# Softmax weights normalised ahead of their transposes, in a two-layer hybrid attention trunk on one core

## The chip, the core and the metric

The kernel is one program on one core of a Trainium2 chip. The metric is the device time of the program in microseconds (us); before the change its median over three runs is 1350.64 us (1348.82 to 1351.12). All times are in us unless marked ns. Engines: PE (TensorE, matrix products and transposes, with PEld its weight loads), DVE (VectorE), ACT (ScalarE), POOL (GpSimd), SP (SyncE, which issues the DMAs).

## What is computed

Two layers over 512 tokens of width 1024. Each layer normalises x, projects it once into the heads of five attention branches (four heads of 64 each), and merges the five results by sigmoid gates. Four branches take a softmax, whose weights are divided by their row sum:

```
e = jnp.where(mask, jnp.exp(l - m), 0.0)
return e / jnp.maximum(jnp.sum(e, axis=-1, keepdims=True), 1e-30)
...
y = (softmax weights) @ v, times the SiLU gate z of the branch
```

A attends to the keys that a top-k leaves, B to all earlier keys with a forget bias, E to 256 memory tokens. D runs three softmaxes (compressed keys, selected blocks, window) and adds their results, each times a sigmoid gate per token and head: `g0*o_cmp + g1*o_slc + g2*o_win`. C is a stick-breaking branch without a softmax; the change doesn't touch it.

## The kernel before

**Stages.** Every layer runs the branches as Python generators that `weave` interleaves with projections and merges, so that PE always has large products beside the attention. In the stretch that matters here the order is: E (`mem_attn`) with the merge of C, the projections of D and the first half of the top-k; D (`nsa_attn`) with the merge of E, the projections of A and the rest of the top-k; A (`dsa_attn`) with the merge of D and B's projections; B (`fox_attn`) with the merge of A; the merge of B alone. The projections and merges write the tile `pj`; their weights come in by DMA (`wraw`), are split by ACT into `whi` (L269) and by DVE into `wlo` (L270), and multiply in three products of 128 by 512 each.

**Order.** A scheduler lays the instructions of each engine out once, when the program is built; on the chip each engine takes its own list strictly in order and waits on semaphores where an operand is not there. A late operand therefore holds everything behind it on that engine.

**A head in a causal branch (A, B, D).** `causal` (L575 on) goes over four blocks of 128 queries and four heads. PE writes the scores into a bank S (two banks). `softmax_p` (L541) then lets DVE add the mask and find the maximum (L546, with its accumulator read), and ACT take the exponential and the row sum (L547, with its accumulator read). Two heads later (`lag` is 2) `finish` transposes the weights P on PE (`pt`, L556), ACT or DVE copy them to SBUF (L537, L539), and after the fourth head `pv_pair` multiplies them with V into a bank Y, which holds features on partitions and tokens on columns.

**Division.** Y is not yet divided. `inv_sums` (L605) takes the reciprocal of the four sums on DVE. They lie one per token on partitions, while Y has tokens on columns, so `head_rows` (L611) spreads them to 256 columns (ACT for A, B and E at L616; DVE for D at L618, times the gate) and transposes them on PE, two transposes into a bank `hr` (L621). `gated_y` (L637) multiplies `hr` by the SiLU gate Z (L640) and Y by that (L642). In D each of two parts (selected, window) has its own Y, `hr`, copy (L1183) and product (L1185); the compressed part comes from two products into a bank `oc`, and three passes of DVE add and gate (L1193 to L1196). Banks Y, `pt`, `hr` and `oc` share three banks (tag T).

**E.** `mem_attn` works on pairs of heads: scores, maximum (L1273), exponential (L1274), transposes and products with V follow at once for each pair.

Of the kernel before, what the change touches and what calls it, by code (L numbers as in the profile page):

```python
# [21 lines left out]
T = 512  # L22
# [164 lines left out]
def trunk(ctx: ExitStack, tc: tile.TileContext, xt, memt, pos, wall, small, vec, ca, cb, out):  # L187
# [373 lines left out]

    def pv_pair(Y, pr, V, PTs, nblk, last):

        after_qk = recent[-1] if last is None else None
        for j in range(nblk):
            for e in (1, 0):
                m = mm(Y[64 * e:64 * e + 64, pr], V(e, j), PTs[e][:, 128 * j:128 * j + 128], j == 0, j == nblk - 1)
                after(m, last, after_qk)
                last, after_qk = m, None
        return last  # L570

    def causal(blocks, lag):

        pend = []
        for i, scores, sums, mask, V, done in blocks:  # L575
            n = 128 * (i + 1)
            st_ = {"P": [], "PT": []}

            share = (4, 2, 1, 1)[i]
            for h in range(4):  # L580
                S = bank("S", "S")
                scores(h, S[:, :max(n, 256)], slice(128 * i, 128 * i + 128), slice(0, max(n, 256)))
                P = softmax_p(S[:, :n], n, mask, sums[:, h:h + 1])

                def finish(i=i, h=h, n=n, P=P, V=V, done=done, st_=st_, share=share):
                    st_["P"].append(P)
                    if len(st_["P"]) == share:
                        PT = transposed(st_["P"], share * (i + 1))
                        st_["PT"] += [PT[:, n * k:n * k + n] for k in range(share)]
                        st_["P"] = []  # L590
                    if h == 3:
                        Y = bank("Y", "T", (128, 2, 128))
                        last = None
                        for pr in (1, 0):
                            last = pv_pair(Y, pr, lambda e, j: V(2 * pr + e, j), st_["PT"][2 * pr:], i + 1, last)
                        done(Y)

                pend.append(finish)
                if len(pend) > lag:
                    pend.pop(0)()  # L600
                yield
        for f in pend:
# [7 lines left out]

    def head_rows(r, gate=None):  # L611

        rb_ = sm.tile([128, 4, 64], F32, name="rb_", bufs=1)
        rr = r[:, :, None].to_broadcast([128, 4, 64])
        if gate is None:
            nc.scalar.activation(rb_, rr, AF.Copy)  # L616
        else:
            nc.vector.tensor_mul(rb_, rr, gate[:, :, None].to_broadcast([128, 4, 64]))  # L618
        p = bank("hr", "T", (128, 2, 128))
# [65 lines left out]
    def layer(l, xs, begin):  # L685
# [122 lines left out]
        def small_proj():  # L808
# [35 lines left out]
            for h in range(4):  # L844
# [5 lines left out]
                for i in range(1, NB):  # L850
# [5 lines left out]
                    else:  # L856
                        R = wk.tile([128, T], F32, name="R", tag="P", bufs=3)[:, :n]
# [72 lines left out]
        def sb_attn(pr):  # L930
# [12 lines left out]
            def begin(e, j):  # L943
# [10 lines left out]
                t = wk.tile([128, T], F32, name="sp_t", tag="P", bufs=3)[:, :w]  # L954
# [90 lines left out]
        def plain_attn(scores, mask, V, Z, Yhl):  # L1045
            def blocks():
                for i in range(NB):
                    sums = sm.tile([128, 4], F32, name="sums", bufs=4)
# [384 lines left out]
```

## Time and profile before

| | |
|---|---|
| median of three runs | 1350.64 us |
| the profiled execution | 1351.01 us |
| its span, first to last instruction | 1349.2 us |
| PE busy | 1310.1 us (97%), 7240 matmul instructions |
| DVE busy | 892.8 us (66%), 1847 |
| ACT busy | 689.0 us (51%), 1300 |
| POOL busy | 11.4 us (1%), 28 |
| granted TensorE clock | 0.997 of full speed, so the 2.4 GHz level |

How to read it: matmuls are pipelined, so the busy time of one overlaps that of the next; what one costs PE is the distance between two starts in the order of time. A wait is the idle time in front of an instruction, put down to what ended it. The chain of work that ended last is followed back from the last instruction.

### The profile page before, as it was taken

What the parts mean: (1) busy time and instruction counts of PE and PEld (TensorE: products, weight loads), DVE (VectorE), ACT (ScalarE), POOL (GpSimd) and SP (SyncE); (2) the same over time, 40 slices, a digit from 0 to 9 for tenths busy, and PEclk for the clock granted to TensorE, in tenths of its full rate; (3) what the DMA queues carried; (4) which work ended last, traced back from release to release, by engine and by line L of the source; (5) the groups of instructions that cost most, each with busy time, mean ns of one, the idle gap of its engine ahead of it and who ended that gap; (6) DMA issues with size and microseconds to landing.
All of it is one profiled execution on the core that took longest, in us unless ns stands there. A gap on an engine that the chain in (4) does not pass through costs nothing.

```text
span 1349.2 us, 18962 instructions
## 1 busy us (share of the span) xinstructions
PE 1310.1 (97%) x7240; PEld 1068.4 (79%) x7240; DVE 892.8 (66%) x1847; ACT 689.0 (51%) x1300; POOL 11.4 (1%) x28
## 2 busy tenths in 40 slices
PE   7999999999999999999999999999999999999997
PEld 6777777878888788878887777777788778887896
DVE  6887999767655444545567799995676463454554
ACT  6887834357545434434447795534574452343340
POOL 0000000000000000000000000000000000000000
PEclk9999999999999999999999999999999999999998
DMA  6442321321123132224524313222122222323231
GB/s 215 139 127 77 110 78 63 94 78 59 63 79 102 55 94 78 71 84 130 183 81 126 109 63 110 85 68 84 57 69 63 86 86 66 100 77 103 94 111 63
DMA packets 40235, 124.11 MB, mean 92 GB/s; under 512 B 4432, under 2 KB 6480, under 8 KB 40144
## 3 DMA queue, kind: packets, MB, share of 16 engines
q1 hardware_dynamic: 40144, 122.89, 28.5%
q8 instruction: 57, 0.93, 0.3%
q14 instruction: 34, 0.28, 0.1%
HBM read 118.16 MB, written 4.72 MB: 91 GB/s over the span
## 4 chain that ended last, share of the span: by engine, by line
PE 70%; ACT 6%; DVE 5%; issue 2%; DVEq 0%; ACTq 0%
PE pj L259 58%; PE Y L259 3%; PE S L259 3%; PE pt L556 3%; ACT whi L269 2%; DVE wlo L270 1%; PE hr L621 1%; ACT sw L430 1%; ACT sw L431 1%; PE sbz L259 1%; DVE P L546 0%; ACT P L547 0%; DVE score L902 0%; DVE m L901 0%; ACT Qi L848 0%
## 5 line engine op out<-in xcount | busy, mean ns | idle before, releaser
L259 PE MATMUL pj<-h_hi,whi 128*128 128x512 f32 x1088 | 429.5, 396 | 0.7 <-DVE rt L433 0.7
L259 PE MATMUL pj<-h_hi,wlo 128*128 128x512 f32 x1088 | 429.0, 394 | 0.0
L259 PE MATMUL pj<-h_lo,whi 128*128 128x512 f32 x1088 | 429.0, 394 | 0.0
L270 DVE TENSOR_TENSOR wlo<-wraw,whi 128x1024 fp32r<-128x1024 f32 x183 | 223.7, 1223 | 228.1 <-ACT whi L269 217.0
L269 ACT ACTIVATE whi<-wraw 128x1024 fp32r<-128x1024 f32 x183 | 193.4, 1058 | 319.9 <-PE pj L259 213.9
L259 PEld LDWEIGHTS pj<-h_hi,wlo 128*128 128x128 f32 x1088 | 204.5, 188 | 42.8 <-DVE wlo L270 2.3
L259 PEld LDWEIGHTS pj<-h_hi,whi 128*128 128x128 f32 x1088 | 204.6, 188 | 40.5 <-issue 1.7
L259 PEld LDWEIGHTS pj<-h_lo,whi 128*128 128x128 f32 x1088 | 204.6, 188 | 40.4 <-issue 1.8
L547 ACT ACTIVATE P<-P,nm 128x128 f32<-128x128 f32 (+3 forms) x128 | 71.6, 559 | 67.7 <-DVE nm L546 64.2
L259 PE MATMUL pj<-yhi,whi 128*128 128x512 f32 (+1 forms) x192 | 71.9, 374 | 2.9 <-ACT yhi L269 2.9
L259 PE MATMUL pj<-yhi,wlo 128*128 128x512 f32 (+1 forms) x192 | 71.6, 373 | 0.0
L259 PE MATMUL pj<-ylo,whi 128*128 128x512 f32 (+1 forms) x192 | 71.5, 372 | 0.0
L556 PE MATMUL pt<-CA,P 128*128 128x128 f32 x384 | 62.7, 277 | 2.6 <-ACT P L1274 1.3
L546 DVE CUSTOM_DVE_ANT_0 P<-S,CA 128x128 f32<-128x128 f32 (+3 forms) x104 | 47.6, 468 | 18.1 <-PE S L259 18.0
L556 PEld LDWEIGHTS pt<-CA,P 128*128 128x128 f32 x384 | 44.9, 141 | 18.2 <-ACT P L1274 6.0
L259 PE MATMUL S<-Ks,Qs 128*128 128x256 f32 (+2 forms) x160 | 51.0, 358 | 6.6 <-DVE nm L546 6.5
L394 ACT ACTIVATE G<-pj 128x512 f32<-128x512 f32 x92 | 53.6, 582 | 0.3
L902 DVE MATCH_REPLACE8 score<-m,score 128x256 f32<-128x256 f32 (+2 forms) x96 | 51.7, 541 | 0.0
L901 DVE MAX8 m<-score 128x8 f32<-128x256 f32 (+2 forms) x96 | 49.7, 546 | 0.0
L799 DVE SCALAR_TENSOR_TENSOR G<-G,pj 128x512 f32<-128x512 f32 x64 | 43.6, 681 | 3.6 <-PE pj L259 3.3
L800 DVE TENSOR_TENSOR acc<-acc,G 128x512 f32<-128x512 f32 x64 | 44.0, 688 | 0.9
L259 PEld LDWEIGHTS pj<-yhi,whi 128*128 128x128 f32 x192 | 36.2, 188 | 10.4 <-ACT yhi L269 4.0
(478 smaller groups left out, 2006.1 us busy)
## 6 DMA issues: line engine op xcount, KB each, us to landing
wraw<-in_wall_dram SPq DMA_DIRECT2D x192, 512.0 KB, 3.7
wc<-in_wall_dram SPq DMA_DIRECT2D x16, 256.0 KB, 6.1
x<-in_xt_dram SPq DMA_DIRECT2D x8, 256.0 KB, 7.0
mraw<-in_memt_dram SPq DMA_DIRECT2D x4, 512.0 KB, 4.7
xo<-in_xt_dram SPq DMA_DIRECT2D x8, 256.0 KB, 4.3
xspill<-xn SPq DMA_DIRECT2D x8, 256.0 KB, 2.2
xo<-xspill SPq DMA_DIRECT2D x8, 256.0 KB, 4.0
out_dram<-o SPq DMA_DIRECT2D x8, 256.0 KB, 2.2
```

The costliest lines, as they stand in the source:

```text
L259: return nc.tensor.matmul(out_, lhsT, rhs, start=start, stop=stop, **kw)
L269: nc.scalar.activation(hi, raw, AF.Copy)
L270: nc.vector.tensor_sub(lo, raw, hi.bitcast(F32))
L394: i = nc.scalar.activation(*a, **k)
L430: nc.scalar.activation(sw[a], p[b], AF.Copy)
L546: nc.vector.tensor_tensor_reduce(P, S, mask, -1.0, 3e38, OP.add, OP.min, nm)
L547: nc.scalar.activation(P, P, AF.Exp, bias=nm, scale=-1.0, accum_out=sums)
L556: nc.tensor.transpose(pt[:, 128 * j:128 * j + 128], x[:, c:c + 128], ident)
L799: nc.vector.scalar_tensor_tensor(G, G, gc, p, op0=gop, op1=OP.mult)
L800: nc.vector.tensor_add(acc, acc, G)
L901: nc.vector.max(m8, lv.work[i])
L902: nc.vector.match_replace(lv.work[i], m8, lv.work[i], REPL)
```

## The change

The division moves from Y to P. In A, B and D each head's weights are multiplied on DVE by the reciprocal of their sum (in D also by the gate of their part), in `normalise` (L594, L595), whose call stands behind the next head's `softmax_p`. `head_rows` goes, with its transposes and the passes that used them. Y is multiplied by Z alone (L648). D's two parts and the compressed part add up in one bank Y, which is taken at the first part and read after the last. In E the weights are multiplied on POOL (L1270), the sums are inverted for two heads at a time, and transposes and products come a pair of heads later. P has four buffers where it had three.

```diff
     def softmax_p(S, n, mask, sums):
-        P = wk.tile([128, T], F32, name="P", tag="P", bufs=3)[:, :n]
+        P = wk.tile([128, T], F32, name="P", tag="P", bufs=4)[:, :n]
...
     def causal(blocks, lag):
-        for i, scores, sums, mask, V, done in blocks:
+        pend, norm_ = [], []
+        for i, parts, rest, done in blocks:
...
+            for b, (scores, mask, V, gate) in enumerate(parts):
+                sums = sm.tile([128, 4], F32, name="sums", bufs=4)
+                for h in range(4):
...
+                    Ps.append(softmax_p(S[:, :n], n, mask, sums[:, h:h + 1]))
+                    if norm_:
+                        norm_.pop()()
+                    def normalise(x=Ps[h], s=sums[:, h:h + 1], g=None if gate is None else gate[:, h:h + 1]):
+                        nc.vector.reciprocal(s, s)
+                        nc.vector.tensor_scalar(x, x, s, g, op0=OP.mult, **({} if g is None else dict(op1=OP.mult)))
+                    norm_.append(normalise)
...
+                            if not more:
+                                if rest is not None:
+                                    rest(st_["Y"], last)
+                                done(st_["Y"])
...
-    def head_rows(r, gate=None):
-        rb_ = sm.tile([128, 4, 64], F32, name="rb_", bufs=1)
...
-        for pr in range(2):
-            nc.tensor.transpose(p[:, pr], rb_[:, 2 * pr:2 * pr + 2].rearrange("p h d -> p (h d)"), ident)
-        return p
...
-    def gated_y(i, Y, r, Z, Yhl):
-        rows = head_rows(r)
-        g = yt("g")
-        nc.vector.tensor_mul(g, rows, Z[:, :, 128 * i:128 * i + 128])
+    def gated_y(i, Y, Z, Yhl):
         y = yt("y")
-        nc.vector.tensor_mul(y, Y, g)
+        nc.vector.tensor_mul(y, Y, Z[:, :, 128 * i:128 * i + 128])
...
         def nsa_attn():
+                    def rest(Y, last, i=i):
+                        for pr in range(2):
+                            m = mm(Y[:, pr], lv.vcb[:, 128 * pr:128 * pr + 128], lv.PC[:, 128 * i:128 * i + 128], False, pr == 1,
+                                   skip_group_check=True)
...
         def mem_attn():
+                    r = inv_sums(sums, 2)
+                    for e in range(2):
+                        x = P[:, NM * e:NM * e + NM]
+                        nc.gpsimd.tensor_scalar(x, x, r[:, e:e + 1], None, op0=OP.mult)
+                    def finish(i=i, pr=pr, P=P, st_=st_):
+                        PT = transposed(P, 4)
...
+                    pend.append(finish)
+                    if len(pend) > 1:
+                        pend.pop(0)()
```

How the instructions move, at three places. First PE in E, first layer, second pair of heads of the second block (S are scores of one head, `pt` takes the transposes of P, `pj` projections). Before, the scores of the pair and what follows:

```order
L259 MATMUL pj_1908<-yhi_1088,wlo_1628 128x512
L259 MATMUL S_1925<-KE_945,Qs_1174 128x256
L259 MATMUL S_1925<-KlE_946,Qs_1174 128x256
L259 MATMUL S_1931<-KE_945,Qs_1177 128x256
L259 MATMUL S_1931<-KlE_946,Qs_1177 128x256
L259 MATMUL pj_1968<-h_hi_384,whi_1964 128x512
L259 MATMUL pj_1968<-h_lo_385,whi_1964 128x512
```

Now, at the same place:

```order
L259 MATMUL pj_1902<-yhi_1088,wlo_1621 128x512
L259 MATMUL S_1920<-KE_945,Qs_1174 128x256
L259 MATMUL S_1920<-KlE_946,Qs_1174 128x256
L259 MATMUL S_1926<-KE_945,Qs_1177 128x256
L259 MATMUL S_1926<-KlE_946,Qs_1177 128x256
L556 MATMUL pt_1937<-CA_95,P_1836 128x128 x4
L259 MATMUL pj_1955<-h_hi_384,whi_1951 128x512
L259 MATMUL pj_1955<-h_lo_385,whi_1951 128x512
```

Before, the transposes of this pair's P_1924 came eleven and twelve projections behind its scores. Now those of the pair before (P_1836) stand there, and those of this pair come 78 projections later.

Second PE in D, first layer, end of a block of two (Y takes the products with V, PC and vcb are the compressed part). Before:

```order
L259 MATMUL S<-Ks,Qs 128x384
L259 MATMUL Y<-PT,VSW 64x128 x8
L621 MATMUL hr<-CA,rb__3318 128x128 x2
L259 MATMUL oc<-PC,vcb 128x128 x2
L259 MATMUL S<-Kl,Qs 128x384
L259 MATMUL S<-Ks,Qs 128x384
L556 MATMUL pt<-CA,P 128x128 x3
L259 MATMUL S<-Kl,Qs 128x384
L556 MATMUL pt<-CA,P 128x128 x3
L259 MATMUL S<-Ks,Qs 128x384
L259 MATMUL S<-Kl,Qs 128x384
```

Now:

```order
L259 MATMUL S<-Ks,Qs 128x384
L259 MATMUL Y<-PT,VSW 64x128 x8
L259 MATMUL Y<-PC,vcb 128x128 x2
L259 MATMUL S<-Kl,Qs 128x384
L556 MATMUL pt<-CA,P 128x128 x3
L259 MATMUL S<-Ks,Qs 128x384
L259 MATMUL S<-Kl,Qs 128x384
L556 MATMUL pt<-CA,P 128x128 x3
```

The two transposes `hr` are gone, and the products that went to `oc` go to Y, right behind its own; the scores and transposes of the next heads follow in nearly the same order.

Third DVE in B, second layer, last block (P<-S is mask and maximum; `wlo`, G and acc belong to weights and merge). Before:

```order
L800 TENSOR_TENSOR acc<-acc,G 128x512
L539 COPY PT<-pt 128x384
L546 ISA P,nm<-S,CA 128x512
L546 ISA nm 128x1
L640 TENSOR_TENSOR g<-hr,Z 128x256
L642 TENSOR_TENSOR y<-Y,g 128x256
L270 TENSOR_TENSOR ylo<-y,yhi 128x2x128
L270 TENSOR_TENSOR wlo<-wraw,whi 128x1024
L799 SCALAR_TENSOR_TENSOR G<-G,pj 128x512
```

Now:

```order
L546 ISA P,nm<-S,CA 128x512
L546 ISA nm 128x1
L806 TENSOR_TENSOR acc<-acc,G 128x512
L539 COPY PT<-pt 128x384
L546 ISA P,nm<-S,CA 128x512
L546 ISA nm 128x1
L594 RECIPROCAL sums<-sums 128x1
L595 TENSOR_SCALAR P<-P,sums 128x512
L594 RECIPROCAL sums<-sums 128x1
L648 TENSOR_TENSOR y<-Y,Z 128x256
L595 TENSOR_SCALAR P<-P,sums 128x512
L270 TENSOR_TENSOR ylo<-y,yhi 128x2x128
```

The product with `hr` is gone; two reciprocals and two scalings stand behind the second head's maximum, ahead of the copies and splits of the merge.

## Rows read from the trace of the kernel before

**Rows 1.** The page, busy time of each engine (share of the span, instructions).

```profile
PE 1310.1 (97%) x7240; PEld 1068.4 (79%) x7240; DVE 892.8 (66%) x1847; ACT 689.0 (51%) x1300; POOL 11.4 (1%) x28
```

**Rows 2.** The page, the chain that ended last, by line.

```profile
PE pj L259 58%; PE Y L259 3%; PE S L259 3%; PE pt L556 3%; ACT whi L269 2%; DVE wlo L270 1%; PE hr L621 1%; ACT sw L430 1%; ACT sw L431 1%; PE sbz L259 1%; DVE P L546 0%; ACT P L547 0%; DVE score L902 0%; DVE m L901 0%; ACT Qi L848 0%
```

**Rows 3.** Waits of PE: us in total, times, longest us.

```profile
PE S L259 <- DVE nm L546: 6.5, 11, 0.9
...
PE pt L556 <- ACT P L1274: 1.3, 2, 0.6
```

**Rows 4.** PE in order of time, behind Y: start us, us, instruction.

```profile
189.58 0.44 PE L621 MATMUL hr<-CA,rb__1951 128*128 128x128 f32 x2
189.77 0.47 PE L259 MATMUL pj<-h_lo,whi 128*128 128x512 f32 x1
```

**Rows 5.** PE in order of time, between projections.

```profile
228.30 0.39 PE L259 MATMUL pj<-h_lo,whi 128*128 128x512 f32 x1
...
228.75 0.39 PE L259 MATMUL pj<-h_hi,whi 128*128 128x512 f32 x1
228.99 0.38 PE L621 MATMUL hr<-CA,rb__2263 128*128 128x128 f32 x2
...
229.44 0.40 PE L259 MATMUL pj<-h_hi,wlo 128*128 128x512 f32 x1
```

**Rows 6.** PE in order of time, ahead of transposes of P.

```profile
317.20 0.44 PE L621 MATMUL hr<-CA,rb__3162 128*128 128x128 f32 x2
317.48 0.38 PE L556 MATMUL pt<-CA,P 128*128 128x128 f32 x2
```

**Rows 7.** Chain in order of time, twelve transposes: start us, us.

```profile
498.17 1.31 PE pt L556 x12
```

**Rows 8.** Groups by line, PE's weight loads: busy us, mean ns | idle before.

```profile
L556 PEld LDWEIGHTS pt<-CA,P 128*128 128x128 f32 x384 | 44.9, 141 | 18.2 <-ACT P L1274 6.0
```

**Rows 9.** Groups by line and form, DVE: busy us, mean ns | idle before.

```profile
L608 DVE RECIPROCAL rsum<-rsum 128x4 f32<-128x4 f32 x40 | 6.9, 171 | 0.8
...
L640 DVE TENSOR_TENSOR g<-hr,Z 128x256 f32<-128x256 f32 x24 | 10.1, 422 | 24.8 <-PE hr L621 24.7
...
L546 DVE CUSTOM_DVE_ANT_0 P<-S,CA 128x512 f32<-128x512 f32 x24 | 16.3, 682 | 7.7 <-PE S L259 7.7
...
L905 DVE TENSOR_SCALAR score<-score 128x512 f32<-128x512 f32 x2 | 0.8, 418 | 0.0
...
L905 DVE TENSOR_SCALAR score<-score 128x256 f32<-128x256 f32 x2 | 0.5, 274 | 0.0
...
L871 DVE TENSOR_SCALAR fu<-v,VEC 32x512 f32<-32x512 f32 x2 | 1.0, 486 | 0.1
```

**Rows 10.** Groups by line and form, ACT.

```profile
L547 ACT ACTIVATE P<-P,nm 128x512 f32<-128x512 f32 x32 | 23.0, 720 | 21.6 <-DVE nm L546 20.7 <-DVE rsum L607 1.0
...
L547 ACT ACTIVATION_READ_ACCUMULATOR P<-P,nm 128x1 f32 x128 | 24.0, 187 | 0.0
...
L1274 ACT ACTIVATE P<-S,nm 128x256 f32<-128x256 f32 x32 | 15.0, 471 | 21.7 <-DVE nm L1273 21.3
```

**Rows 11.** Busy time by stretch: length, PE, PEld, DVE, ACT, POOL, clock, DMA.

```profile
150.00:200.00 50.00, 49.60 (x312) 37.63 (x311) 48.82 (x119) 24.46 (x48) 0.00 (x0) 1.00 0.32 105
...
450.00:500.00 50.00, 49.71 (x288) 42.38 (x288) 18.77 (x31) 17.73 (x30) 0.00 (x0) 1.00 0.21 64
```

**Rows 12.** Groups by line, DVE, 150 to 250 us alone.

```profile
L902 DVE MATCH_REPLACE8 score<-m,score 128x512 f32<-128x512 f32 (+2 forms) x45 | 24.2, 542 | 0.0
...
L270 DVE TENSOR_TENSOR wlo<-wraw,whi 128x1024 fp32r<-128x1024 f32 x13 | 15.8, 1218 | 0.4
L1273 DVE TENSOR_REDUCE nm<-S 128x1 f32<-128x256 f32 x14 | 5.6, 414 | 0.6 <-PE S L259 0.5
```

**Rows 13.** Groups by line, POOL.

```profile
L476 POOL MEMSET Ks<- 64x512 f32 x16 | 8.7, 545 | 932.5 <-PE S L259 389.8 <-DVE sq L683 386.7 <-issue 61.1
L476 POOL MEMSET KlE<- 64x256 f32 x8 | 2.4, 306 | 15.2 <-ACT sq L336 8.4 <-DVE h_lo L270 6.5
```

More of the change, by code (lines that the diff above doesn't have):

```diff
@@ L560, in transposed, with pv_pair @@
         return o
-    def pv_pair(Y, pr, V, PTs, nblk, last):
-        after_qk = recent[-1] if last is None else None
+    def pv_pair(Y, pr, V, PTs, nblk, last, hold, first, end):
         for j in range(nblk):
             for e in (1, 0):
-                m = mm(Y[64 * e:64 * e + 64, pr], V(e, j), PTs[e][:, 128 * j:128 * j + 128], j == 0, j == nblk - 1)
-                after(m, last, after_qk)
-                last, after_qk = m, None
+                m = mm(Y[64 * e:64 * e + 64, pr], V(e, j), PTs[e][:, 128 * j:128 * j + 128], first and j == 0, end and j == nblk - 1,
+                       skip_group_check=True)
+                after(m, last, hold)
+                last, hold = m, None
@@ L570, in pv_pair @@
         return last
     def causal(blocks, lag):
-        pend = []
-        for i, scores, sums, mask, V, done in blocks:
+        pend, norm_ = [], []
+        for i, parts, rest, done in blocks:
             n = 128 * (i + 1)
-            st_ = {"P": [], "PT": []}
+            st_ = {"Y": None}
             share = (4, 2, 1, 1)[i]
[L580 to L601, printed above, removed]
@@ L602, in causal, with finish @@
-        for f in pend:
+            for b, (scores, mask, V, gate) in enumerate(parts):
+                sums = sm.tile([128, 4], F32, name="sums", bufs=4)
+                Ps = []
+                pt_ = {"P": [], "PT": []}
+                for h in range(4):
+                    S = bank("S", "S")
+                    scores(h, S[:, :max(n, 256)], slice(128 * i, 128 * i + 128), slice(0, max(n, 256)))
+                    Ps.append(softmax_p(S[:, :n], n, mask, sums[:, h:h + 1]))
[5 more added lines that the diff above has]
+                    norm_.append(normalise)
+                    def finish(i=i, h=h, b=b, n=n, Ps=Ps, V=V, rest=rest, done=done, st_=st_, pt_=pt_, share=share, more=b + 1 < len(parts)):
+                        pt_["P"].append(Ps[h])
+                        if len(pt_["P"]) == share:
+                            PT = transposed(pt_["P"], share * (i + 1))
+                            pt_["PT"] += [PT[:, n * k:n * k + n] for k in range(share)]
+                            pt_["P"] = []
+                        if h == 3:
+                            if st_["Y"] is None:
+                                st_["Y"] = bank("Y", "T", (128, 2, 128))
+                            last = st_.get("last")
+                            hold = recent[-1]
+                            for pr in (1, 0):
+                                last = pv_pair(st_["Y"], pr, lambda e, j: V(2 * pr + e, j), pt_["PT"][2 * pr:], i + 1, last, hold,
+                                               b == 0 and pr == 1, not more and rest is None and pr == 0)
+                                hold = None
+                            st_["last"] = last
+                            if not more:
[3 more added lines that the diff above has]
+                    pend.append(finish)
+                    if len(pend) > lag:
+                        pend.pop(0)()
+                    yield
@@ L603, in causal @@
+        for f in norm_ + pend:
             f()
@@ L1047, in blocks @@
                 for i in range(NB):
-                    sums = sm.tile([128, 4], F32, name="sums", bufs=4)
-                    yield i, scores, sums, mask(i), V, lambda Y, i=i, sums=sums: gated_y(i, Y, inv_sums(sums, 4), Z, Yhl)
+                    yield i, [(scores, mask(i), V, None)], None, lambda Y, i=i: gated_y(i, Y, Z, Yhl)
             yield from causal(blocks(), 2)
@@ L1202, in nsa_attn @@
+                    yield i, parts, rest, lambda Y, i=i: gated_y(i, Y, lv.ZD[0], lv.YD)
             yield from causal(blocks(), 2)
```

69 lines of the change are left out of this document (24 added, 45 removed).

## The prediction

> **What bounds the kernel now.** I read the page's busy times first: PE is busy for 1310.1 of 1349.2 us, DVE for two thirds [rows 1]. A busy PE is not yet a bound, so the chain comes next: its longest items are projections on PE (58%), with other products of PE behind them, and `hr`, the transposes that the change removes, has a line of its own with 1% [rows 2]. Then the waits of PE: the largest ones in the attention stages are scores that wait for DVE to free their bank, 6.5 us in 11 waits, and transposes that wait for an exponential, 1.3 us [rows 3]. So PE has work nearly all the time, an instruction less on PE is time off the span, and what other engines do counts only where PE comes to wait for it. The sum is made against the profiled execution, 1351.0 us, which lies 0.4 us above the median of the three runs; I treat the two as one.
>
> **What goes from PE.** Forty pairs of transposes go: four blocks, in A, B, E once and in D twice, in two layers. A matmul's own duration (0.27 to 0.33) overlaps its neighbours', so I take distances between starts, and these depend on what stands around a pair. Behind Y and ahead of a projection, the projection starts 0.19 us after the pair [rows 4]. Between projections, two steps that take 0.45 us elsewhere take 0.69, so 0.24 for the pair [rows 5]. Ahead of the transposes of P, 0.28 [rows 6]. Counted in PE's order before: 10 pairs of the first kind, 9 of the second, 11 of the third; 8 stand ahead of `oc` and 2 ahead of other such products, which I price as the third. 10 x 0.19 + 9 x 0.24 + 21 x 0.28 = **10.0 us**. From below: twelve transposes in a row take 1.31 us, 0.109 each [rows 7], so 80 are worth 8.7. The products into `oc` stay, under the name Y; that they now always follow Y I count at nothing.
>
> **Moved: E's transposes.** A pair of heads' first transposes came 0 to 18 projections behind its last scores; in the new order it is 26 to 78. Before, exponential and read (0.47 + 0.19) [rows 10] and the maximum in front stood in that gap, and PE paid for the narrow ones. PE's own waits of this kind are 1.3 us [rows 3]; the weight loads idled 6.0 us for the same reason [rows 8], part of it while PE still worked off the matmul in front. I take **-1.3 us** and keep 6.0 as the far end. The products with V come later too; only Y and the merge of E wait for them, and that merge runs in the next stage.
>
> **Added on DVE.** 128 reciprocals at 0.17 and 128 scalings: 0.42 at 512 columns, 0.27 at 256, about 0.31 as a mean of the four widths [rows 9]. The rows take constants; one with a pointer scalar took 0.49 at 512 [rows 9], the upper end. That is 22 + 40 = 62 us, and 16 small inversions of sums in E instead of 8, 3 us more. Off go 72 passes of 256 columns (24 times `hr` by Z, and in D 16 spreads, 16 products and 16 additions) at 0.42, 30 us, and 32 inversions of two instructions, 11 us. DVE gains some 24 us of work, nearly all in D, A and B. There it is far from full: in 450 to 500 us it works 18.8 us of 50 [rows 11]. As work this costs nothing. If DVE were full there, as it is in E, all 24 us would be on the path.
>
> **The new wait.** In A, B and D a head's transposes now wait for its scaling. Queued behind them on PE are the next scores and the projections. The chain from scores to transposes at 512 columns was 0.68 on DVE and 0.72 + 0.19 on ACT [rows 9, 10]; now 0.17 + 0.42 come on top: 2.2 us, with a short read of DVE's accumulator and the hand-overs beside. Against it stands the distance in the new order, counted at 0.225 us a projection [rows 5]: most heads have 4 us or more, since the scaling is issued ahead of the long stretch of merge. Nine of 128 have under 3.3; six of them, A's last block in both layers, 2.0 to 2.9. A head loses nothing at best and the added 0.6 us at worst. Half of it for nine heads is **+3 us** (0 to 5.4).
>
> **E's scaling on POOL.** 32 instructions of 128 by 256. The trace has no POOL instruction that reads; the nearest are fills of 64 partitions, 0.31 us at 256 columns and 0.55 at 512 [rows 13]. Reading and writing at the slower fill's pace gives 1.09 for the far end, 0.31 the near one; I take 0.55, one read and one write at the short fill's pace. In the gap of at least 26 projections, 5.9 us, stand 0.41 + 0.47 + 0.19 [rows 10, 12], two small instructions of DVE at 0.17 and two on POOL: 2.5 us at 0.55, 3.6 at 1.09. It fits with 2 us to spare for DVE's queue, so **0**. The fourth buffer of P, the fewer passes of ACT and the unused `hr` banks free things that PE hardly waits for: 0. No DMA is added or moved past another; SP's list changes only with the scheduler's order.
>
> **Sum.** 1351.0 - 10.0 - 1.3 + 3.0 = **1342.7 us**.
>
> **Rivals.** *The scores' waits double.* DVE gets two more instructions per head between the maxima that free the two banks S. Today PE waits 6.5 us for this; if the waits double where heads come close together, 1342.7 + 6.5 = 1349.2. For it: D has 32 heads a layer, and at some places scores and transposes alternate without projections. Against it: in the order shown for B the scalings stand behind both maxima, not between them. 0.14.
>
> *POOL holds DVE up in E, and PE with it.* DVE works 48.8 of 50 us there [rows 11], a quarter of it on one of the two instructions of a top-k step (24.2 us in 100), 15.8 in 100 on the two-operand passes for `wlo` [rows 12], which with the smaller passes of that kind make about a quarter too. If every scaling on POOL stopped DVE for its length, and PE was as late as DVE, 32 x 0.55 = 17.6 us: 1360.3. It decides from 8.3 us that reach PE; above that the kernel is slower than before. For it: DVE has no idle time to catch up with before the stage ends. Against it: the top-k is not wanted until A, and weights are split ahead of use. 0.13. The Trainium skill (SBUF — State Buffer, Who interferes with whom) speaks for this rival: VectorE and GpSimd share a pair of SBUF ports, and an instruction of VectorE with two SBUF inputs waits for a GpSimd instruction that reads. By its rule only the quarter of DVE's work with two SBUF inputs is hit, an estimate of 4.4 us if all of it reaches PE, so 1347.1; no run here shows it yet.
>
> *The change doesn't free what it removes.* If something other than PE sets the pace, say weights that come late through ACT and DVE, the 10 us turn into waits and the time stays 1351. Against it: PE idles 0.3 to 0.4 us in 50 [rows 11]. 0.07.
>
> **How the numbers follow.** The forecast has 0.66. About 0.2% of the time, 2.7 us, is what a measurement of this kernel can tell from no change. The forecast and a mild form of the first rival (0.04, up to 1347.9) are faster: 0.70. The rest of that rival and the third are no change: 0.10 + 0.07 = 0.17. The second is slower: 0.13. The range begins where the transposes go with the whole 6.0 us of idle loads and no new wait comes, 1351.0 - 16.0 = 1335, and ends above the first rival's time, at 1350.5; outside it are the second rival and most of the third.
>
> **What the profile after would show.** Right: no `hr` line, 80 matmuls fewer; PE busy some 10 us lower with the span; waits of `pt` for the scaling (L595) of a few us, mostly in A; POOL's 32 scalings under 1.1 us each; transposes in E that wait for nothing. Wrong: waits of scores or `pt` on DVE of over 10 us; POOL scalings over 1.6 us; `wlo` passes stretched beside POOL, and projections waiting for them in E; or PE as busy as before with more idle time in front of `pj`.

## The result and the profile after

The changed kernel takes 1337.97 us (median of four runs, 1336.52 to 1339.09), the kernel before 1350.13 (four runs now, 1348.82 to 1351.12): a ratio of 0.9909 with a 95% interval of 0.9897 to 0.9921, 12.2 us less. The forecast was 1342.7, in a range of 1335.0 to 1350.5: the right sign and the right bound, 4.7 us too careful, with errors in its terms that in part cancel. The profiled execution of the changed kernel took 1338.58 us, its span is 1336.8.

First the page of the changed kernel, busy times and the chain by line, to be read beside [rows 1, 2]:

```profile
PE 1299.8 (97%) x7160; PEld 1066.1 (80%) x7160; DVE 916.1 (69%) x1983; ACT 675.0 (50%) x1260; POOL 42.5 (3%) x60
...
PE pj L259 67%; PE Y L259 4%; PE S L259 3%; PE pt L556 3%; ACT whi L269 2%; PE sbz L259 1%; DVE wlo L270 1%; ACT sw L430 1%; ACT Qi L854 1%; ACT sw L431 1%; ACT sp_t L388 1%; DVE Kl L456 0%; DVE rt L435 0%; DVE sw L434 0%; DMA wraw<-in_wall_dram 0%
```

PE has 80 instructions less, is busy for 10.3 us less, and the span fell by 12.4 us. `hr` is gone from the chain. PE still has work for 97% of the span, so the bound is the same engine with less to do.

The waits of PE after (us in total, times, longest), beside [rows 3]:

```profile
PE S L259 <- DVE nm L546: 4.0, 5, 1.5
...
PE pt L556 <- DVE P L595: 2.3, 3, 1.5
PE pj L259 <- ACT yhi L269: 2.3, 2, 1.3
PE Y L259 <- ACT PT L537: 1.6, 4, 0.7
...
PE Y L259 <- DVE PT L539: 1.0, 2, 0.6
```

The wait that the change adds is there, 2.3 us in three places; E's wait of 1.3 us for exponentials is gone; and the scores wait 4.0 us for their banks where they waited 6.5. The products with V wait 2.6 us for the copies of their transposes (PT), where it was 0.9 before.

Where in the program the time went can be read from PE's order of time: the moment at which the last product of each branch with V starts, in us from the start of the span.

| last product of | before | after | gained so far | gained in the stretch |
|---|---|---|---|---|
| C, layer 1 | 154.9 | 154.0 | 0.9 | 0.9 (start of the program) |
| D (with E before it) | 380.6 | 376.6 | 4.0 | 3.1 |
| A | 504.4 | 500.0 | 4.4 | 0.4 |
| B | 576.4 | 572.1 | 4.3 | -0.1 |
| C, layer 2 | 814.6 | 809.4 | 5.2 | 0.9 |
| D (with E) | 1043.1 | 1033.1 | 10.0 | 4.8 |
| A | 1165.1 | 1154.0 | 11.1 | 1.1 |
| B | 1238.3 | 1226.8 | 11.5 | 0.4 |
| end of the span | 1349.2 | 1336.8 | 12.4 | 0.9 |

The start, up to C, holds nothing of the change but a fourth buffer for a pass of C (`sp_t`), which shares the buffers of P; among the kernels below the time to the first product of C lies between 95.9 and 98.8 us without any pattern, so 0.9 of the 12.4 is such scatter. E and D give 7.9 us, with 24 of the 40 pairs of transposes; A gives 1.5 and B 0.3, with 8 pairs each. E and D are taken together because in the new order E's last products run in D's time.

### The profile page after: what moved, and what is told of

The parts are those of the page before. It is cut to its first block, busy times and chain, and to the rows that moved or that the text cites. A ratio compares the mean times of both kernels' runs of the same rounds, so it can differ in the third digit from the quotient of the medians.

```text
span 1336.8 us, 18894 instructions
## 1 busy us (share of the span) xinstructions
PE 1299.8 (97%) x7160; PEld 1066.1 (80%) x7160; DVE 916.1 (69%) x1983; ACT 675.0 (50%) x1260; POOL 42.5 (3%) x60
## 4 chain that ended last, share of the span: by engine, by line
PE 81%; ACT 9%; DVE 6%; issue 3%; DMA 1%; SPq 0%; DVEq 0%; ACTq 0%
PE pj L259 67%; PE Y L259 4%; PE S L259 3%; PE pt L556 3%; ACT whi L269 2%; PE sbz L259 1%; DVE wlo L270 1%; ACT sw L430 1%; ACT Qi L854 1%; ACT sw L431 1%; ACT sp_t L388 1%; DVE Kl L456 0%; DVE rt L435 0%; DVE sw L434 0%; DMA wraw<-in_wall_dram 0%
```

## The experiments

Two kernels weigh the transposes, two split the change, three vary the scaling, three vary how far a head may run ahead, one takes the scaling away, one puts the old chain back at one place.

**hr_twice.** The kernel before, every pair of transposes issued twice:

```diff
-        for pr in range(2):
-            nc.tensor.transpose(p[:, pr], ...)
+        for _ in range(2):
+            for pr in range(2):
+                nc.tensor.transpose(p[:, pr], ...)
```

> The kernel before, with each of the 40 pairs of transposes of the spread reciprocals issued twice into the same bank; nothing else is added. Theory (PE's list is the time, a pair costs what its distances between starts show): 80 more transposes cost 8.7 us by their bare spacing and 10.0 us by the local distances, so 1358.8 to 1360.1 us where the kernel before has 1350.1. Rival (PE's small instructions hide in waits that are there anyway, and the change gained by moving waits): under 3 us more.

Measured: 1356.67 us (1356.11 to 1357.38), ratio 1.0048 (1.0035 to 1.006), 6.6 us more than the 1350.07 of the kernel before. For 40 pairs that is 0.165 us each. Pairs do cost PE time one by one, but less than the 0.25 that the forecast had as a mean. The second pair stands directly behind the first. In the trace it moves what follows by 0.22 us, the bare spacing of [rows 7], wherever the order behind it is the same in both kernels. That would be 8.7 us for 40 pairs; about 2 of them don't reach the end, and most of this is lost in E and D, which take 3.5 us more for their 24 pairs. Which waits take it up there is not shown.

**hr_back.** The changed kernel, with 40 pairs of transposes put back behind the products with V. They transpose a constant into a bank that nobody reads:

```diff
+    def spare(last):
+        p = bank("hr", "T", (128, 2, 128))
+        for pr in range(2):
+            after(nc.tensor.transpose(p[:, pr], ident, ident), last)
...
+                            spare(last)
...
+                            spare(st_["last"])
```

> The changed kernel, with 40 pairs of transposes put back behind the products with V; they transpose a constant and nobody reads the result, so no work of DVE or ACT comes back. Theory: 8.7 to 10.0 us more than the changed kernel's 1338.0, so 1346.7 to 1348.0; the 2 to 4 us that remain of the gain are other things (waits, switches between kinds of products). Rival: the time stays within 3 us of 1338.0.

Measured: 1344.83 us (1343.1 to 1345.58), ratio 0.9959 (0.9947 to 0.9972), 6.9 us more than the changed kernel: 0.17 a pair. The two traces show what a pair adds at one and the same place. D's compressed products behind Y and the scores that follow, in the changed kernel:

```profile
298.40 0.71 PE L259 MATMUL Y<-PC,vcb 128*128 128x128 f32 x4
298.87 0.36 PE L259 MATMUL S<-Ks,Qs 128*128 128x256 f32 x1
```

With the pair put back:

```profile
299.62 0.44 PE L576 MATMUL hr<-CA 128*128 128x128 f32 x2
299.90 0.61 PE L259 MATMUL Y<-PC,vcb 128*128 128x128 f32 x4
300.27 0.36 PE L259 MATMUL S<-Ks,Qs 128*128 128x256 f32 x1
```

The next product starts 0.28 us after the pair, as in [rows 6], but the scores then come 0.37 us behind it, where it is 0.47 without a pair. So the pair moves them by 0.18. The same is seen at the other places: ahead of projections the next start moves by 0.19 and the fourth by 0.16, ahead of transposes of P by 0.28 and 0.22 (medians of the places with the same order in both). With 0.16 for 21 pairs, 0.17 for D's 8 and 0.22 for the 11 ahead of transposes the sum is 7.1 us, and 6.9 were measured. So of the 12.2 us, some 7 are the transposes themselves, and about 5 come from something else.

**causal_only** and **e_only.** The change in A, B and D alone, with E as before and four buffers of P; and E alone, with the rest as before and three buffers of P. The diffs are the two halves of the change.

> The change in A, B and D alone; E is as before, with its division behind the products (8 of the 40 pairs, no work on POOL). Theory: E's part is worth its 8 pairs, 2.0 us, and the waits for exponentials, 1.3 us: 1338.0 + 3.3 = 1341.3. Rival (E's part gains by its longer lead, up to the 6 us for which weight loads idled): up to 1346. Rival (POOL holds DVE up in E): 1338 or below.

> The change in E alone, with three buffers for P; A, B and D are as before. Theory: 1350.1 - 3.3 = 1346.8. Rival (the longer lead is the larger part): 1342 to 1344. Rival (POOL and DVE hold each other up): 1350 or above.

Measured: 1341.35 us (1340.08 to 1342.0), ratio 0.9931 (0.9917 to 0.9945), 8.7 us less than before; and 1347.27 (1346.49 to 1348.89), ratio 0.9981 (0.9972 to 0.9989), 2.8 us less. Together 11.5 of 12.2: the halves add up within what a measurement can tell. E's 2.8 us fit its 8 pairs at 0.17 (1.4 us) and the wait of 1.3 us that went [rows 3].

**pool_twice.** The changed kernel with a second pass on POOL in E, by a column of ones:

```diff
                         nc.gpsimd.tensor_scalar(x, x, r[:, e:e + 1], None, op0=OP.mult)
+                        nc.gpsimd.tensor_scalar(x, x, ones1, None, op0=OP.mult)
```

> The changed kernel, with every scaling on POOL in E followed by a second one of the same size, by one: 32 POOL instructions more, at 0.99 us each as measured. Theory (the 26 or more projections between scores and transposes hold it): a pair's chain grows by 2 us; within 2 us of the changed kernel's 1338.0. Rival (POOL holds DVE up in E and PE with it): 32 x 0.99 = 31.8 us more POOL time stops DVE; a quarter of that, 8 us, to all of it, reaches PE: 1346 or above, and wlo passes stretch beyond 1.22 us.

Measured: 1349.14 us (1347.5 to 1351.55), ratio 0.9992 (0.9983 to 1.0), 11.2 us more than the changed kernel. The theory that POOL has room to spare fell. Groups of POOL by line (busy us, mean ns), and the new wait of PE, in this kernel:

```profile
L1271 POOL TENSOR_SCALAR P<-P,ones 128x256 f32<-128x256 f32 x32 | 32.8, 1037 | 0.0
L1270 POOL TENSOR_SCALAR P<-P,rsum 128x256 f32<-128x256 f32 x32 | 31.3, 990 | 350.0 <-ACT Ks L486 218.0 <-DVE rsum L630 96.9 <-PE Y L259 20.0
```

```profile
PE pt L556 <- POOL P L1271: 7.7, 10, 1.6
```

One pass takes 0.99 us, not 0.55. A pair of heads needs two, and two more in this kernel, so some 2 us come on top of the chain ahead of E's transposes, and that is too much for the narrowest places: PE waits ten times. All of the 11.2 us arise in E and D (228.5 and 229.1 us for the two layers, 222.6 and 223.7 in the changed kernel); the new wait sums to 7.7, and in E of the first layer PE also has a stretch at a lower clock that the changed kernel hasn't (a mean of 0.50 from 216 to 218 us). It is in the main lateness, not a slower DVE: the mean of the passes for `wlo` stays at 1223 ns here, as it was before, and the few passes that meet a scaling (shown further down) don't change that.

**e_on_dve.** E's scaling on DVE instead of POOL:

```diff
-                        nc.gpsimd.tensor_scalar(x, x, r[:, e:e + 1], None, op0=OP.mult)
+                        nc.vector.tensor_scalar(x, x, r[:, e:e + 1], None, op0=OP.mult)
```

> The changed kernel, with E's 32 scalings on DVE instead of POOL (0.35 us each as DVE's scalings of 256 columns measured). DVE has under 1 us of 50 idle in that stage, so 11.2 us of work are added to a full engine. Theory (only what PE comes to wait for counts; top-k has room until A): within 2 us of 1338.0. Rival (DVE is the bound of the stage): half of it to all of it, 1343.6 to 1349.

Measured: 1336.83 us (1336.43 to 1339.96), ratio 0.9902 (0.9889 to 0.9916), the same as the change. The row of the pass in this kernel, and of the pass in the changed one:

```profile
L1270 DVE TENSOR_SCALAR P<-P,rsum 128x256 f32<-128x256 f32 x32 | 9.9, 346 | 0.0
```

```profile
L1270 POOL TENSOR_SCALAR P<-P,rsum 128x256 f32<-128x256 f32 x32 | 31.4, 994 | 368.2 <-ACT Ks L486 218.1 <-DVE rsum L630 110.0 <-PE Y L259 21.8
```

DVE does in 0.35 us what POOL does in 0.99. Even in E, where DVE has hardly any idle time [rows 11], 9.9 us more of work on it did not reach PE. POOL was not needed for this.

**at_once.** The scaling written right behind its own `softmax_p`, not a head late:

```diff
-                    if norm_:
-                        norm_.pop()()
...
-                    norm_.append(normalise)
+                    normalise()
```

> The changed kernel, with each head's reciprocal and scaling written right behind its own softmax in A, B and D, not behind the next head's. The scheduler still places them. Theory (the distance from scores to transposes decides, not the place in the program): within 1.5 us of 1338.0. Rival (a scaling that waits for its exponential stands ahead of the next head's maximum on DVE, so scores wait for their bank): each of 128 heads may add the exponential's 0.75 us to DVE's line, and where 1 in 10 reaches PE that is 10 us: about 1348.

Measured: 1337.77 us (1336.13 to 1338.71), ratio 0.99 (0.9885 to 0.9915): the same. "A head late" in the code is worth nothing here.

**p3.** The changed kernel with three buffers of P, as before the change (`bufs=4` to `bufs=3`). Two other passes share these buffers and lose one too: one behind the top-k's scores (`R`) and one of C (`sp_t`).

> The changed kernel with three buffers for P, as before the change. Theory: P is held longer now, by the scaling and, in E, by a pair of heads; the masks of the next head then wait for transposes. 1 to 4 us more than 1338.0. Rival (the fourth buffer is not used): same, within 1 us.

Measured: 1341.17 us (1340.38 to 1343.58), ratio 0.9933 (0.9921 to 0.9946), 3.2 us more than with four. Here is a part of the missing 5 us, one that the prediction had counted at nothing. Of it 2.1 us arise in E and D (223.1 and 225.2 us for the two layers against 222.6 and 223.7), and the scores wait 6.0 us in this kernel, nearly what they waited before [rows 3]:

```profile
PE S L259 <- DVE nm L546: 6.0, 9, 1.5
```

The code suggests how: the pass that adds the mask and finds the maximum writes into P, and P is in use until its transposes, two heads later, are done. With three buffers a new head's maximum waits for a buffer, and PE for the bank that this maximum frees. PE's waits for `R` and `sp_t` are as long as with four (0.4 us, and 1.2 against 1.3), so nothing points at those two.

**p5.** Five buffers (`bufs=5`).

> The changed kernel with five buffers of P in place of four. Three buffers cost 3.2 us over four (1341.17 against 1337.97). Theory: what the fourth buffer gave is a limit on how far scores run ahead of transposes, and with four that limit is nearly off, since the waits left are 4.0 us for maxima and 2.3 us for scalings: 1337.5 to 1338.5, the same as the change. Rival: each further buffer lets the scheduler place scores earlier, and another 2 to 3 us go: 1335 to 1336.

Measured: 1337.49 us (1337.02 to 1338.76), ratio 0.9908 (0.9895 to 0.9922): the same as four, as the theory had it.

**p5_lag3.** Five buffers, and the transposes of a head in A, B and D three heads behind its scores:

```diff
-            yield from causal(blocks(), 2)
+            yield from causal(blocks(), 3)
```

> Five buffers of P, and in A, B and D the transposes of a head come three heads behind its scores in place of two. Theory: the new wait of transposes for the scaling (2.3 us) goes, and with it nothing else, since PE has hardly any other idle time in these stages; the products with V at the end of each branch come in one lump more: 1335.5 to 1337.5. Rival: the lag costs more at the end of each branch (three heads without other work behind the last scores) than the wait was worth: 1338.5 to 1341.

Measured: 1334.46 us (1333.04 to 1335.35), ratio 0.9884 (0.987 to 0.9897): 3.5 us under the changed kernel, 15.8 under the one before, and faster than either. The theory had 1335.5 to 1337.5 and expected the wait for scalings to go. That wait hardly changed in the sum, from 2.3 to 2.1 us; the scores' wait for maxima fell from 4.0 to 2.4. By the moments of the table A and B together take 192.1 us in the first layer, where they take 194.9 in p5, and 191.8 against 193.7 in the second, of which the stretch behind B gives 0.8 back.

The clearest place is in A of the first layer, where the scores of the last block are written. There no projections are left to stand between the heads. PE in order of time in the changed kernel (start us, us, what it waited for), from the second block's products with V on; `pt` are transposes of the third block:

```profile
438.28 1.09 PE L259 MATMUL Y<-PT,VA 128*64 128x128 f32 x16 [0.59 <-DVE PT L539]
...
440.91 0.52 PE L556 MATMUL pt<-CA,P 128*128 128x128 f32 x3 [0.59 <-DVE P L595]
...
443.93 0.52 PE L556 MATMUL pt<-CA,P 128*128 128x128 f32 x3 [1.53 <-DVE P L595]
...
446.63 0.78 PE L259 MATMUL fox_e<-chi,sel 128*128 128x512 f32 x1
```

The same stretch with a lag of three heads:

```profile
438.27 1.09 PE L259 MATMUL Y<-PT,VA 128*64 128x128 f32 x16
...
442.48 0.55 PE L556 MATMUL pt<-CA,P 128*128 128x128 f32 x3 [0.62 <-DVE P L595]
443.02 0.50 PE L259 MATMUL fox_e<-chi,sel 128*128 128x512 f32 x1
```

From Y to the first `fox_e` (a product for B that comes next) it takes 8.35 us in the one and 4.75 in the other. PE's waits are 2.95 us of the one and 0.86 of the other. The rest is not all gain: with a lag of three the scores of two of the last block's four heads stand outside this stretch.

The same `fox_e` also takes 0.78 in the one and 0.50 in the other. Busy time by stretch shows the clock behind it (length, PE, PEld, DVE, ACT, POOL, granted clock, DMA). The kernel before:

```profile
441.00:445.00 4.00, 2.60 (x26) 1.79 (x25) 3.97 (x10) 1.94 (x5) 0.00 (x0) 1.00 0.42 131
445.00:449.00 4.00, 2.93 (x18) 1.82 (x17) 3.64 (x9) 3.07 (x7) 0.00 (x0) 1.00 0.22 66
```

The changed kernel:

```profile
441.00:445.00 4.00, 2.23 (x10) 1.09 (x10) 3.58 (x13) 1.95 (x6) 0.00 (x0) 1.00 0.25 66
445.00:449.00 4.00, 4.00 (x15) 3.21 (x15) 2.88 (x11) 2.91 (x8) 0.00 (x0) 0.57 0.00 0
```

With a lag of three heads:

```profile
441.00:445.00 4.00, 3.13 (x19) 2.43 (x19) 4.00 (x14) 3.55 (x9) 0.00 (x0) 1.00 0.00 0
445.00:449.00 4.00, 4.00 (x36) 4.00 (x35) 1.98 (x5) 0.98 (x3) 0.00 (x0) 1.00 0.02 4
```

In the changed kernel PE is busy for 2.23 of 4 us, and right behind that it runs most of the next 4 us at the lower of its two levels, 1.2 GHz (a mean of 0.57); up to 4 x 0.43 = 1.7 us are lost to that where PE is the bound. From the first `fox_e` to the projections behind it takes 1.84 us here and 1.03 with a lag of three. With three buffers (p3) the means are 0.50 and 0.70 from 445 to 449 and from 449 to 453 us. Before the change, and with a lag of three, PE stays at 2.4 GHz through A.

In the second layer such a stretch follows in A too, and there it costs nothing. The kernel rows_b (below) differs from the changed one only in the last blocks of B; in A its order is the same, and in its profiled execution the clock stayed up at that place. First the changed kernel, then rows_b:

```profile
1098.00:1100.00 2.00, 2.00 (x7) 1.20 (x6) 1.87 (x8) 1.79 (x5) 0.00 (x0) 0.50 0.38 121
```

```profile
1098.00:1100.00 2.00, 1.36 (x6) 0.61 (x5) 1.87 (x8) 1.81 (x6) 0.00 (x0) 1.00 0.39 115
```

From the second block's products with V to the first `fox_e` both take 8.80 us (from 1092.67 to 1101.47 and from 1092.69 to 1101.49): slower products of PE fill time in which it waits otherwise. The four runs of the changed kernel fit a small price of the clock, without proving it: mean clocks of 0.997, 0.995, 0.995 and 0.992 go with 1336.52, 1337.37, 1338.58 and 1339.09 us.

**no_scale.** The changed kernel without reciprocals and scalings in A, B and D, so that their weights are not divided by their sums (in D also not gated):

```diff
-                        nc.vector.reciprocal(s, s)
-                        nc.vector.tensor_scalar(x, x, s, g, op0=OP.mult, **({} if g is None else dict(op1=OP.mult)))
+                        return
```

> The changed kernel without the reciprocals and the scalings in A, B and D, so that the weights of these branches are not divided by their sums; E is left as it is. It measures what the added work on DVE costs in all. Theory: only the new wait of the transposes, 2.3 us in the waits of PE, and some of the 4.0 us of scores that wait for maxima: 1334.5 to 1336. Rival: DVE's 72 us more in D, A and B reach PE by other ways too (weights split later, banks freed later): below 1333. Second rival: the wait is taken back a few instructions further on, and nothing is gained: 1337.5 to 1338.5.

Measured: 1336.96 us (1334.48 to 1337.38), ratio 0.9899 (0.9886 to 0.9913), 1.0 us under the changed kernel, which is less than can be told from no change. 72.5 us of passes on DVE and the whole new wait are gone, and nearly nothing is gained. The waits of PE in this kernel say why:

```profile
PE S L259 <- DVE nm L546: 6.7, 9, 1.7
...
PE pt L556 <- ACT P L547: 0.7, 3, 0.3
```

Transposes that wait no more let the next scores come earlier, and these wait for DVE's maxima, 6.7 us instead of 4.0. In the last block of A, Y to `fox_e` takes 8.56 us instead of 8.35, and the stretch at the lower clock is longer than with the scaling (means of 0.50 and 0.72 from 445 to 449 and from 449 to 453 us). The time lies between the theory's range and the second rival's, in neither; the waits show the second rival's mechanism: what the transposes no longer wait, the scores wait a few instructions further on.

**rows_b.** The changed kernel with the old passes put back behind the products of B's last block alone (the copy spreads ones, so the values stay as they are):

```diff
+            nc.scalar.activation(rb_, ones1[:, :, None].to_broadcast([128, 2, 128]), AF.Copy)
+            p = bank("hr", "T", (128, 2, 128))
+            for pr in range(2):
+                after(nc.tensor.transpose(p[:, pr], rb_[:, pr], ident), tail[0])
+            g = yt("g", 1)
+            nc.vector.tensor_mul(g, p, Z[:, :, 128 * i:128 * i + 128])
+            nc.vector.tensor_mul(y, Y, g)
...
```

> The changed kernel with, in the last block of B alone, the passes of the old chain put back between Y and the merge: a copy of ones, two transposes behind the products with V, their product with Z on DVE and that of Y with it. It tests whether the chain from Y to the last merge is shorter by what the traces show (4.30 us from Y to the first projection on yhi before, 3.39 after). Theory: two pairs of transposes at 0.16 us and about 0.9 to 1.4 us of the chain in each layer, 2.1 to 3.1 us in all: 1340.1 to 1341.1. Rival: PE fills that gap with other work, and only the pairs count: 1338.3.

Measured: 1340.13 us (1338.35 to 1342.39), ratio 0.9927 (0.9913 to 0.994), 2.2 us more than the changed kernel; of the profiled spans 1.5 us, all of it behind the last product of the second layer (111.5 us against 109.9 to the end). The timeline shows the chain there. In the kernel before:

```profile
1236.64 1.97 PE L259 MATMUL Y<-PT,VB 128*64 128x128 f32 x32
...
1238.54 0.44 PE L621 MATMUL hr<-CA,rb__11590 128*128 128x128 f32 x2
...
1239.02 0.42 DVE L640 TENSOR_TENSOR g<-hr,Z 128x256 f32<-128x256 f32 x1 [2.50 <-PE hr L621]
...
1240.48 0.40 ACT L269 ACTIVATE yhi<-y 128x256 fp32r<-128x256 f32 x1
...
1240.94 0.50 PE L259 MATMUL pj<-yhi,whi 128*128 128x512 f32 x1 [1.27 <-ACT yhi L269]
```

In the changed kernel:

```profile
1225.13 1.97 PE L259 MATMUL Y<-PT,VB 128*64 128x128 f32 x32
...
1227.14 0.42 DVE L648 TENSOR_TENSOR y<-Y,Z 128x256 f32<-128x256 f32 x1 [2.16 <-PE Y L259]
...
1228.06 0.41 ACT L269 ACTIVATE yhi<-y 128x256 fp32r<-128x256 f32 x1
...
1228.52 0.50 PE L259 MATMUL pj<-yhi,whi 128*128 128x512 f32 x1 [0.99 <-ACT yhi L269]
```

With the old passes back:

```profile
1225.17 1.97 PE L259 MATMUL Y<-PT,VB 128*64 128x128 f32 x32
...
1227.07 0.44 PE L656 MATMUL hr<-CA,rb__11485 128*128 128x128 f32 x2
...
1229.93 0.50 PE L259 MATMUL pj<-yhi,whi 128*128 128x512 f32 x1 [2.19 <-ACT yhi L269]
```

From the products to the first projection on their result it takes 4.30 us before, 3.39 after and 4.76 with the passes back; PE waits 1.27, 0.99 and 2.19 us of that. So the theory holds in the second layer, though the chain put back is 0.46 us longer than the old one was. In the first layer the passes cost nothing: there the projection waits for ACT, which takes up `yhi` 3.45 us after Y starts in the changed kernel and 3.63 with the passes back, and the stretch is as long with them as without (183.8 and 183.7 us). In the kernel before ACT takes it up 4.31 us after Y starts. A pass for `whi` stands ahead of it on ACT, and starts 3.35 us after Y before the change, 2.49 after it and 2.70 with the passes back. So this kernel did not put back the delay of the first layer; what held `whi` before is not shown.

## Why the prediction was right, point by point

**Right in kind: PE is the bound, so what leaves PE leaves the span.** Transposes that only PE misses were worth time in both directions, 6.6 us for 40 more and 6.9 us for 40 put back. The third rival, that nothing is freed, is excluded by that.

**The first term was too big.** The prediction took 10.0 us, with 8.7 as the least. The runs give 6.6 to 6.9, 0.165 to 0.17 a pair. The step that failed is "I take distances between starts", read up to the next start alone: that next product and the ones behind it win a part back. Ahead of D's compressed products, 8 places at the price of "the third" kind, the distance is 0.28 as in [rows 6] and the pair adds 0.17; ahead of transposes of P it is 0.28 and 0.22, behind Y and ahead of projections 0.19 and 0.16. Pairs between two projections, 9 before the change, have no counterpart in the kernel that puts pairs back. The lower bound, 0.109 a transpose [rows 7], is what a pair adds where it stands behind other transposes, and is not a least elsewhere. That a matmul costs PE the distance between two starts, as the part ahead of the prediction has it, holds only over several starts.

**Terms counted at nothing that weren't.** *The fourth buffer of P* "frees things that PE hardly waits for: 0": it is worth 3.2 us. The prediction had the row that spoke for it, 6.5 us of scores that wait for DVE [rows 3], and asked only whether these waits would grow. *Fewer passes behind Y*: the prediction counted passes as DVE's work, and so at nothing, but at the end of B nothing else is left for PE, and there they stand on the path: 0.9 us by the table in the last stretch, which the kernel that puts the passes back confirms with 1.5, from a chain longer than the old one. The table shows another 0.9 us behind B in the first layer, where the first projection on `yhi` starts 4.77 us after Y before the change and 3.90 after it; that no run puts back.

**E's moved transposes** were to give 1.3 us. The wait is gone, and E alone gives the 2.8 us of 8 pairs and this wait. Right, by size too. The far end, the 6.0 us of idle weight loads [rows 8], did not come.

**The new wait** was to cost 3.0 us (0 to 5.4). It shows as 2.3, in three places, all of them in A, as forecast, though at transposes of its third block. One of the three is 1.53 us, where the prediction had 0.6 as the worst for a head. But a wait shown is not a cost: without the scaling the time is the same within 1.0 us, since the scores' wait for maxima grows in its place. Against that stands a price that the prediction did not have, the stretches at half the clock behind those waits: at most 1.7 us in A of the first layer, and nothing in the second, by the comparison with rows_b. What they cost in the first layer stays open: no run removes them there and leaves the rest. The lag of three heads removed them in A together with much of that block's waiting, worth 3.0 us over the same kernel with a lag of two.

**DVE's work.** Reciprocals were forecast at 0.17 and scalings at 0.31 in the mean. In the changed kernel (groups by line and form, busy us and mean ns):

```profile
L594 DVE RECIPROCAL sums<-sums 128x1 f32<-128x1 f32 x128 | 19.9, 158 | 8.1 <-ACT P L547 7.5
...
L595 DVE TENSOR_SCALAR P<-P,sums,gt 128x512 f32<-128x512 f32 x16 | 8.7, 543 | 0.3
...
L595 DVE TENSOR_SCALAR P<-P,sums 128x512 f32<-128x512 f32 x16 | 7.6, 483 | 0.3
...
L595 DVE TENSOR_SCALAR P<-P,sums,gt 128x128 f32<-128x128 f32 x16 | 5.5, 344 | 0.2
...
L595 DVE TENSOR_SCALAR P<-P,sums 128x128 f32<-128x128 f32 x16 | 4.4, 286 | 0.4
```

The eight forms of scalings sum to 52.6 us, 0.41 each: the end that the prediction named and did not take, the 0.49 of a pointer scalar [rows 9], was the right one at 512 columns. It changed nothing, because DVE has that time in D, A and B. Its busy time grew by 23.3 us, near the forecast's 24, but not for its reason: the durations of its instructions grew by 34 in the sum, and neighbours overlap in time.

**POOL** was taken at 0.55 us, with bounds of 0.31 and 1.09. It measured 0.99 in the mean, near the far end. The term stayed 0 as the prediction had said it would at that end (3.6 us of 5.9), and pool_twice shows how little room was left.

**The sum with the measured sizes:** 6.8 for the pairs, 1.3 for E's wait, 3.2 for the buffer, 1.8 behind B in the two layers, 0.9 of scatter at the start, 0.5 for scores that wait 6.0 and not 6.5 us even with three buffers, less 2.3 for the new wait: 12.2 us, where the two profiled spans differ by 12.4. This is a reckoning of parts that touch each other, not a proof: the buffer's 3.2 holds some of the lower clock, the pairs at the end of B are in the 6.8 and in the 1.8, the 2.3 is taken off whole although no_scale finds at most 1.0 of it, the longer wait of the products with V is left out, and the shared bank of D with its products into Y was not tried by itself. That the forecast came within 4.7 us is in part luck: the first term was some 3.2 us too large, and the buffer that it left out was worth 3.2.

**The rivals.** *The scores' waits double*: they fell, from 6.5 to 4.0 us. *POOL holds DVE up in E, and PE with it*: with the scaling on DVE the time is the same, so POOL cost nothing. The two engines do hold each other up where they meet, but they seldom meet. A scaling in the changed kernel and the pass `Kl`, with two inputs in SBUF, that starts 0.12 us into it; then the same pass before the change:

```profile
160.25 0.93 POOL L1270 TENSOR_SCALAR P<-P,rsum 128x256 f32<-128x256 f32 x1
160.37 0.90 DVE L456 TENSOR_TENSOR Kl<-rt,Ks 64x512 fp32r<-64x512 f32 x1
```

```profile
160.37 0.68 DVE L456 TENSOR_TENSOR Kl<-rt,Ks 64x512 fp32r<-64x512 f32 x1
```

The other way round, a scaling that starts 0.10 us into such a pass:

```profile
210.60 0.69 DVE L458 SCALAR_TENSOR_TENSOR Qs<-rt,Qs 64x512 fp32r<-64x512 f32 x1
210.70 1.38 POOL L1270 TENSOR_SCALAR P<-P,rsum 128x256 f32<-128x256 f32 x1
```

And in pool_twice the one `wlo` pass that starts early in a scaling:

```profile
256.42 0.92 POOL L1271 TENSOR_SCALAR P<-P,ones 128x256 f32<-128x256 f32 x1
256.60 1.37 DVE L270 TENSOR_TENSOR wlo<-wraw,whi 128x1024 fp32r<-128x1024 f32 x1 [0.87 <-ACT whi L269]
```

`Kl` takes 0.90 us instead of 0.68, and `wlo` 1.37 where its mean is 1.22; the scaling takes 1.38 where most take 0.93. The Trainium skill (SBUF — State Buffer, Who interferes with whom) has a VectorE instruction with two SBUF inputs contend with a GpSimd instruction that reads SBUF; the trace agrees, for `Kl` and for `wlo`. But the wait of DVE's pass is short: 0.21 us for the one that starts 0.12 us into the scaling, 0.15 for the one that starts 0.18 us into it, not the scaling's 0.9. And of the 36 `wlo` passes from 140 to 270 and from 800 to 930 us in the changed kernel none starts in the first 0.9 us of a scaling. So of the 4.4 us that the prediction worked out from that rule only some 0.7 came, on DVE (0.6 of them in the eight passes of `Kl`, whose mean rose from 685 to 761 ns), and none is seen on PE.

## What to carry to other kernels

Where one engine is busy for 97% of the time, price what leaves it by a run that puts it back or doubles it: the distance to the next start is too much where the instructions behind win a part of it back. Ask of every wait on that engine what sets it, the number of buffers and the lag between heads too, and not only whether it will grow. And look first where a branch ends and no other work is left: a shorter chain or one head more of lag counted there, while a wait taken away between heads came back here a few instructions later under another name. And before an engine is said to slow another, look whether their instructions meet in time at all.

## What the runs showed of the hardware that was not expected

- On POOL a 128 by 256 fp32 pass with a scalar per partition takes 0.93 us in the median (0.99 in the mean, 1.51 at most), on DVE 0.35.
- A pass of DVE with two inputs in SBUF that starts 0.12 us into such a pass of POOL is delayed by 0.21 us, one that starts 0.18 us into it by 0.15; a pass of POOL that starts 0.10 us into one of DVE's takes 1.38 us in place of 0.93.
- A pair of small transposes puts the next product off by 0.19 to 0.28 us, and those behind it by 0.16 to 0.22.
- A second scalar per partition in such a pass on DVE costs 0.06 us, at 512 columns (543 against 483 ns) as at 128 (344 against 286).
- A few microseconds in which PE waits several times can be followed by some at 1.2 GHz (a granted clock of 0.57 in the mean of 4 us), which the table of waits does not show. It doesn't follow each time: in the kernel before PE was busy for 2.60 and 2.93 of two stretches of 4 us in the same block, and the clock stayed at 2.4 GHz; and one and the same order of instructions had 0.50 in one execution and 1.00 in another, and took 8.80 us in both.
